# Output projection of a conv decoder block: a tile's three products become a 512- and a 256-column one, and VectorE adds the halves

## The chip, the cores and the metric

The kernel runs on one core of a Trainium2 chip, in one launch. The metric is the device time of that launch in microseconds; several runs of the kernel are timed, and their median counts. One further execution is taken by the hardware profiler, and all rows below are from it.

## The reference, cut to what matters

One decoder layer over 256 tokens of width 2048, in float32. The condition c gives six modulation vectors (sh1, sc1, g1, sh2, sc2, g2). The part that the change touches is the end of the convolution mixer and the start of the second normalisation:

```
u = jax.nn.silu(_layer_norm(u, ln_g, ln_b))
y = u @ w_out + b_out
x = x + (1.0 + g1[:, None, :]) * y
h = _rms_norm(x, norm2_g[i]) * (1.0 + sc2[:, None, :]) + sh2[:, None, :]
u = jnp.square(jax.nn.relu(h @ mlp_w1[i]))
x = x + (1.0 + g2[:, None, :]) * (u @ mlp_w2[i])
```

## The kernel before

**Precision.** A float32 product is made of three products in a reduced float32 format (F32R). Weights and activations are both split into a high part, a rounded copy, and a low part, the remainder: high x high, high x low and low x high are added up. ScalarE makes the high part of the weights (L236), VectorE or GpSimd the low part (L240). A weight tile is 128 x 128; a split works on half of 16 such tiles at a time, and six buffers each are there for high and low halves (`hi`, `lo`). The activations lie as `hl`, channels on the partitions, with the 256 tokens' high parts in columns 0 to 255 and their low parts in 256 to 511.

**Stages.** The kernel goes through a list of jobs: 16 jobs ("in", i) of the input projection with the convolution, 8 jobs ("out", i) of the output projection, and then the feed-forward part in four quarters of jobs ("up", ...), ("down", ...). A job ("out", i) makes the output channels of two tiles, c = 0 and c = 1, and for each of them runs over 16 tiles k of the inner dimension.

**Products.** `mm` has two forms. The plain one (L268, L269) makes a 512-column product of the high weights with high and low activations side by side, and a 256-column product of the low weights with the high activations; the sum then lies in two halves of 256 columns that have yet to be added. The merged one (L264 to L266) makes three 256-column products into the same 256 columns. Job ("out", 0) has a form of its own (`mm_pair`, L283 to L286), jobs 1 to 7 are merged, and job ("up", 0, 0) is plain with `xa` in place of `hl`.

**Accumulators.** PSUM tiles come from named pools: `acc` and `mm` have two buffers each, `small` and `row` one each. A buffer of `acc` holds 512 columns. In jobs 1 to 7 it holds both tiles c of one job.

**What follows an output job.** ScalarE scales each tile by 1 + g1 and adds the bias `gb` = (1 + g1) b_out (L1419), VectorE adds the pair to x (L1420), ScalarE squares the new x (L1422) and scales it by the second norm's factors (L1431), and `split_act` splits the result for the first "up" job (ScalarE L251, VectorE L254). GpSimd sums the squares (L1427).

**Other work of the stage.** After each job stand 1 to 3 columns of the modulation (sh2, L665: two products of 128 x 1024 with an accumulated sum; others L669) on VectorE. Their second half reads a copy of the condition in PSUM that ScalarE makes (L1441). GpSimd makes the low weight parts for jobs 0 to 5, VectorE those for 6 and 7. The first "up" job also has 64 small products (L600) into `row`, ahead of its last two k.

**Order.** Each engine has one queue and takes its instructions in the order written. A scheduler sets that order from its own estimate of the times and from priorities (`urgent()`) and explicit constraints (`tc.issue_after`). Loads of weights and modulation rows are issued by SyncE into seven buffers `raw`, each as soon as its buffer is free.

Of the kernel before, what the change touches and what calls it, by code (L numbers as in the profile page):

```python
# [9 lines left out]
F32 = mybir.dt.float32  # L10
F32R = mybir.dt.float32r
AF = mybir.ActivationFunctionType
ALU = mybir.AluOpType
PSUM = bass.MemoryType.PSUM

P = 128
T = 256
# [18 lines left out]
SH1, SC1, G1, SH2, SC2, G2 = range(6)  # L36
# [51 lines left out]
def conv_block(ctx: ExitStack, tc: tile.TileContext, x, vec, dwq, c_row, mod_r, mod_t, mod_c, w_first, w_in, w_out, w1, w2, out):  # L88
    nc = tc.nc
# [6 lines left out]
    ps = ctx.enter_context(tc.tile_pool(name="ps", bufs=2, space=PSUM))  # L96
# [17 lines left out]
    xs = start_pool.tile([P, KT, T], F32, name="x0")  # L114
# [16 lines left out]
    for i in range(2):  # L131
        p = ps.tile([P, 2, 2 * T], F32, name="mm", bufs=2)
# [6 lines left out]
    state = {"used": 0}  # L139
# [3 lines left out]
    amps = {w: const.tile([P, KT], F32, name=f"amp{w}") for w in (SC1, SC2)}  # L143
# [8 lines left out]
    def urgent():  # L152
        return tc.high_priority(offset=URGENT)

    HALF = KT // 2
# [100 lines left out]
    def mm(p, c, key, acts_of, ks=range(KT), merged=False):  # L256
        halves = parts[key]
        for k in ks:
            hi, lo = halves[k // HALF]
            m = acts_of[k // 2][:, k % 2, :]  # L260
            if merged:
                out_p, begin, end = p[:, c, 0:T], k == 0, k == KT - 1
                w = hi[:, k % HALF, :]
                nc.tensor.matmul(out_p, w, m[:, 0:T], start=begin, stop=False)  # L264
                nc.tensor.matmul(out_p, w, m[:, T : 2 * T], start=False, stop=False)  # L265
                state["mm_end"] = nc.tensor.matmul(out_p, lo[:, k % HALF, :], m[:, 0:T], start=False, stop=end)  # L266
                continue
            nc.tensor.matmul(p[:, c, :], hi[:, k % HALF, :], m, start=(k == 0), stop=(k == KT - 1))  # L268
            state["mm_end"] = nc.tensor.matmul(  # L269
                p[:, c, T : 2 * T], lo[:, k % HALF, :], m[:, 0:T], start=False, stop=(k == KT - 1),  # L270
                skip_group_check=True,
            )
# [25 lines left out]
    def mm_tokens(sums, job, acts_of, last):  # L298
        steps = [(k, r) for k in range(HALF) for r in sums]
        if last:  # L300
            steps = [(k, r) for r in sums for k in range(HALF)]
        for k, (t, cs, p) in steps:
            hi, lo = [w[:, 4 * (k % 2) : 4 * (k % 2) + 4, :].rearrange("p k n -> p (k n)")[:, cs]
                      for w in parts[job + (k // 4,)][k // 2 % 2]]
            at = HALF * (job[2] % 2) + k
            m = acts_of[at // 2][:, at % 2, :]
            shared = job[0] == "down" and job[1] in EIGHT
            begin, end = at == 0 or shared and job[2] == 1 and t == 1 and at == HALF, at == KT - 1
            p_hi, p_lo = [m[:, n : n + P] for n in (t * P, T + t * P)]
            nc.tensor.matmul(p, p_hi, hi, start=begin, stop=False, skip_group_check=shared)  # L310
            nc.tensor.matmul(p, p_hi, lo, start=False, stop=False, skip_group_check=shared)  # L311
            nc.tensor.matmul(p, p_lo, hi, start=False, stop=end, skip_group_check=shared)  # L312

    def run_tasks():
        state["job"] += 1
        with tc.issue_after(state["w_lo"]), tc.issue_after(state["w_hi"]):
            for task in tasks.pop(state["job"], []):
                task()
# [371 lines left out]
    def mcol(which, k):  # L690
        return modc[:, which * KT + k : which * KT + k + 1]
# [21 lines left out]
    def ps_two():  # L713
        return ps.tile([P, 2, T], F32, name="acc", bufs=2)

    def two():
        return tmp.tile([P, 2, T], F32, name="two", bufs=6)

    def pair_of(tiles, k2):
        if tiles is xs:  # L720
            return xs[:, 2 * k2 : 2 * k2 + 2, :]
        return tiles[k2 // 2][:, 2 * (k2 % 2) : 2 * (k2 % 2) + 2, :]
# [4 lines left out]
    hl = [None] * HALF  # L727
# [81 lines left out]
    def splits(job):  # L809
        if job[0] == "eight":  # L810
            with urgent():
                split_eight(*job[1:])
            return
        if job[0] == "seven":
            with urgent():
                split_seven(*job[1:])
            return
        for c in range(2):
            if job + (c,) in parts_early:
                continue  # L820
            on_pool = job[0] == "in" or job in POOLED
            with urgent(), behind(c):
                split_w(job + (c,), nc.gpsimd if on_pool else nc.vector)
            if c == 0:
                state["next_hi"] = state["w_hi"]
                if job[0] in ("up", "down"):
                    with urgent():
                        run_tasks()

    def evac(p, cs=slice(0, 2), out=None):  # L830
        t1 = two()[:, cs, :]
# [7 lines left out]
    p = ps.tile([P, 512], F32, name="small", bufs=1)  # L839
# [10 lines left out]
    with urgent():  # L850
        part = two()[:, 0, :]
        nc.scalar.activation(part, p[:, 0:T], AF.Copy)
        p = ps.tile([P, 512], F32, name="row", bufs=1)
# [8 lines left out]
    for _ in range(2):  # L862
        p = ps.tile([P, 2, 2 * T], F32, name="mm", bufs=2)
# [52 lines left out]
    for k in range(KT):  # L916
        c = k % 2
# [261 lines left out]
    for n, job in enumerate(jobs):  # L1179
# [16 lines left out]
        kind, i = job[0], job[-1]  # L1196
# [32 lines left out]
                    top_up()  # L1229
            continue  # L1230
        if kind == "out" and i > 0:
            p = ps_two()
        elif not by_tokens(job):
            p = ps.tile([P, 2, 2 * T], F32, name="mm", bufs=2)
        if by_tokens(job) and (i % 2 == 0 or kind == "down" and job[1] in EIGHT and i < 4):
# [2 lines left out]
        if job == ("up", 0, 0):  # L1238
            mm(p, 0, job + (0,), xa, range(SIDE))
            for at in range(2 * UNSCALED):  # L1240
                shift_row(at, shown.pop(("up", 0, at // 2, at % 2)))
            fold_shift()
            mm(p, 0, job + (0,), xa, range(SIDE, KT))
            mm(p, 1, job + (1,), xa)
        elif job == ("out", 0):
            for k2 in range(HALF):
                with tc.issue_after(state["row_end"].ins) if k2 == 1 else ExitStack():
                    mm_pair(p, job, k2)
                if k2 == 0:
                    with tc.issue_after(state["mm_end"].ins):  # L1250
                        mod_chunk(*last_row[0][1:], last_row[1])
        elif job in K_OUTER:
            for k2 in range(HALF):
                for c in range(2):
                    mm(p, c, job + (c,), xa if plain else hl, range(2 * k2, 2 * k2 + 2))
        elif kind == "in":
            rows = [key for key in after[job] if key[0] != "col"] if i < KT - 1 else []
            for c in range(2) if i < KT - 1 else (1, 0):
                for ks in (range(HALF), range(HALF, KT)):
                    with tc.issue_after(state.pop("rows_end")) if "rows_end" in state else ExitStack():  # L1260
                        mm(p, c, job + (c,), hl, ks, i == KT - 1)
            if not CONV_AT.get(n):
                with tc.issue_after(state["mm_end"].ins):
                    mods(rows)
                state["rows_end"] = state["row_end"].ins
        elif by_tokens(job):
            mm_tokens(sums[kind, i // 2], job, u2 if kind == "down" else hl, n == len(jobs) - 1)
        else:
            for c in range(2):
                mm(p, c, job + (c,), hl, merged=kind == "out")  # L1270
        with tc.issue_after(state["mm_end"].ins) if kind == "in" else ExitStack():
            mod_finish()
        if n == KT - 3:
# [9 lines left out]
        if kind == "in":  # L1283
# [67 lines left out]
            gb = x_pool.tile([P, KT], F32, name="gb")  # L1351
# [18 lines left out]
            for k2 in range(HALF):  # L1370
# [17 lines left out]
                with urgent():  # L1388
                    nc.gpsimd.tensor_tensor(e, pair_of(cvs, k2), spread(mu), op=ALU.subtract)
                    state["e_end"] = nc.vector.tensor_tensor(e, e, spread(r), op=ALU.mult).ins  # L1390
                    for c in range(2):
                        k = 2 * k2 + c
# [17 lines left out]
        if kind == "out":  # L1410
            if i == 0:
                xs = take(("x", 0))
            t2 = p[:, :, 0:T]
            xp = pair_of(xs, i)
            with urgent():
                for c in range(2):
                    k = 2 * i + c
                    with tc.issue_after(state["next_hi"]) if i == HALF - 2 else ExitStack():
                        nc.scalar.activation(t2[:, c, :], t2[:, c, :], AF.Identity, scale=mcol(G1, k), bias=gb[:, k : k + 1])  # L1419
                nc.vector.tensor_tensor(xp, t2, xp, op=ALU.add)  # L1420
            ss = two()
            nc.scalar.activation(ss, xp, AF.Square)  # L1422
            if i == 0:
# [1 line left out]
            elif i < HALF - 1:  # L1425
                for c in range(2):
                    nc.gpsimd.tensor_tensor(sqacc, sqacc, ss[:, c, :], op=ALU.add)  # L1427
            a = two()
            for c in range(2):
                k = 2 * i + c  # L1430
                nc.scalar.activation(  # L1431
                    a[:, c, :], pair_of(xs, i)[:, c, :], AF.Copy, scale=amps[SC2][:, k : k + 1]
                )
            xa[i] = mp.tile([P, 2, 2 * T], F32R, name="u2", bufs=HALF)
            split_act(xa[i], a)
            if i == IN_PSUM[0]:
# [21 lines left out]
        elif kind == "up":  # L1458
# [7 lines left out]
            if plain:  # L1466
                with urgent():
                    t2 = evac(p)
                    a = two()
# [7 lines left out]
            elif not by_tokens(job):  # L1477
                with urgent():
                    t2 = evac(p)
                    a = two()  # L1480
# [115 lines left out]
```

## Time and profile before

| | |
|---|---|
| time, median of 3 runs | 1066.34 us (1066.32 to 1066.46) |
| the profiled execution's own time | 1066.46 us |
| its span, first to last instruction | 1064.7 us |
| TensorE / VectorE / ScalarE / GpSimd busy | 98% / 86% / 56% / 21% |
| mean granted TensorE clock | 0.997 |

The output jobs take some 85 us of the span, from about 297 to 381 us. A row of the time lines gives the start and length in microseconds; equal instructions in a row are merged (x4), and the time that the engine was idle before it stands in brackets with what ended it. The length of one instruction overlaps the next, so the pace is read from start to start.

### The profile page before, as it was taken

The page shows a single profiled execution, that of the slowest core. Times are in us where ns is not written, and L with a number is a line of the kernel's source. Part 1 is how long each engine was busy: PE and PEld are TensorE (multiplying, and loading weights), DVE is VectorE, ACT ScalarE, POOL GpSimd, SP SyncE. Part 2 cuts the span into 40 slices and gives each one's busy share as a digit, 9 for nine tenths or more (in the row PEclk, how much of TensorE's full clock was granted, in tenths as well). Part 3 has the DMA queues.
Part 4 walks back from the last instruction along what each step waited for, and adds up shares of the span by engine and source line. Part 5 has one row for each costly group of instructions (what it writes and reads, how often), then busy time and mean ns, then how long its engine had stood idle before and what let it go on. Part 6 is the DMA issues. An engine that isn't in the chain of part 4 may idle for free.

```text
span 1064.7 us, 15463 instructions
## 1 busy us (share of the span) xinstructions
PE 1046.3 (98%) x5776; PEld 865.1 (81%) x5776; DVE 911.7 (86%) x1191; ACT 601.5 (56%) x831; POOL 222.3 (21%) x153
## 2 busy tenths in 40 slices
PE   6999999999999999999999999999999999999998
PEld 3888886678699988888888888888888888888886
DVE  5777789998766889878799899899999899899996
ACT  4111298866775585344546565745566744656751
POOL 0000078989689272000000000000000000000001
PEclk8999999999999999999999999999999999999999
DMA  9999997996999976999996998693989796899853
GB/s 381 421 420 420 415 419 315 356 396 237 404 399 406 409 259 261 322 312 327 320 327 248 340 277 271 240 388 108 366 244 321 249 335 179 290 282 347 216 148 59
DMA packets 154333, 330.99 MB, mean 311 GB/s; under 512 B 88465, under 2 KB 114321, under 8 KB 119313
## 3 DMA queue, kind: packets, MB, share of 16 engines
q1 hardware_dynamic: 153248, 328.30, 85.1%
q0 software_dynamic: 864, 1.57, 1.1%
q8 instruction: 45, 0.74, 0.3%
q14 instruction: 30, 0.25, 0.1%
q10 hardware_dynamic: 146, 0.13, 0.0%
HBM read 313.71 MB, written 17.83 MB: 311 GB/s over the span
## 4 chain that ended last, share of the span: by engine, by line
PE 83%; DMA 10%; DVE 5%; ACT 1%; issue 1%; SPq 0%; DVEq 0%; ACTq 0%
PE mm L311 12%; PE mm L312 12%; PE mm L310 12%; DMA raw<-mod_c 9%; PE mm L268 6%; PE mm L269 3%; PE acc L265 3%; PE acc L264 3%; PE acc L266 3%; PE mm L1094 2%; PE row L576 2%; PE acc L485 2%; PE acc L486 2%; PE acc L484 1%; DVE raw L669 1%; DVE lo L240 1%
## 5 line engine op out<-in xcount | busy, mean ns | idle before, releaser
L236 ACT ACTIVATE hi<-raw 128x1024 fp32r<-128x1024 f32 x374 | 383.9, 1055 | 257.7 <-PE mm L312 127.6
L240 DVE TENSOR_TENSOR lo<-raw,hi 128x1024 fp32r<-128x1024 f32 x313 | 371.0, 1217 | 52.4 <-ACT hi L236 51.8
L240 POOL TENSOR_TENSOR lo<-raw,hi 128x1024 fp32r<-128x1024 f32 x61 | 155.8, 2581 | 30.1 <-ACT hi L236 29.8
L669 DVE SCALAR_TENSOR_TENSOR raw<-raw,cond 128x2048 f32<-128x2048 f32 x50 | 117.7, 2356 | 25.2 <-DMA raw<-mod_c 25.2
L460 POOL DMA_DIRECT2D out<-two x6 | 5.4, 902 | 639.2 <-DVE two L458 629.8
L311 PE MATMUL mm<-lo,u 128*128 128x512 f32 x320 | 124.5, 389 | 0.0
L312 PE MATMUL mm<-hi,u 128*128 128x512 f32 x320 | 124.0, 389 | 0.0
L310 PE MATMUL mm<-hi,u 128*128 128x512 f32 x320 | 123.8, 389 | 0.0
L310 PE MATMUL mm<-hi,hl 128*128 128x512 f32 x288 | 112.1, 389 | 0.0
L312 PE MATMUL mm<-hi,hl 128*128 128x512 f32 x288 | 112.1, 389 | 0.0
L311 PE MATMUL mm<-lo,hl 128*128 128x512 f32 x288 | 112.1, 389 | 0.0
L973 DVE SCALAR_TENSOR_TENSOR acc<-u,v,acc 128x256 f32<-128x256 f32 x230 | 91.5, 482 | 0.0
L268 PE MATMUL mm<-hl,hi 128*128 128x512 f32 x256 | 91.1, 399 | 0.0
L269 PE MATMUL mm<-hl,lo 128*128 128x256 f32 x256 | 71.7, 280 | 0.0
L310 PEld LDWEIGHTS mm<-hi,u 128*128 128x128 f32 x320 | 60.1, 188 | 12.6
L312 PEld LDWEIGHTS mm<-hi,u 128*128 128x128 f32 x320 | 60.1, 188 | 12.4
L311 PEld LDWEIGHTS mm<-lo,u 128*128 128x128 f32 x320 | 60.1, 188 | 12.4
L877 PE MATMUL mm<-two,first 128*128 128x256 f32 x240 | 56.7, 391 | 8.5 <-ACT two L935 8.5
L264 PE MATMUL acc<-hl,hi 128*128 128x256 f32 x224 | 63.4, 283 | 0.0
L265 PE MATMUL acc<-hl,hi 128*128 128x256 f32 x224 | 63.4, 283 | 0.0
L266 PE MATMUL acc<-hl,lo 128*128 128x256 f32 x224 | 63.4, 283 | 0.0
L310 PEld LDWEIGHTS mm<-hi,hl 128*128 128x128 f32 x288 | 54.1, 188 | 11.3
(383 smaller groups left out, 2018.8 us busy)
## 6 DMA issues: line engine op xcount, KB each, us to landing
raw<-w SPq DMA_DIRECT2D x128, 1024.0 KB, 7.6
raw<-mod_c SPq DMA_DIRECT2D x64, 1024.0 KB, 11.5
raw<-mod_r SPq DMA_DIRECT2D x28, 1024.0 KB, 8.7
raw<-w_in SPq DMA_DIRECT2D x16, 1024.0 KB, 10.6
raw<-w_out SPq DMA_DIRECT2D x16, 1024.0 KB, 8.2
first<-w_first SPq DMA_DIRECT2D x15, 1024.0 KB, 19.8
u<-kept SPq DMA_DIRECT2D x24, 512.0 KB, 7.6
flat<-two SPq DMA_DIRECT2D x30, 256.0 KB, 7.8
```

The costliest lines, as they stand in the source:

```text
L236: state["w_hi"] = nc.scalar.activation(hi, w[:, ks, :], AF.Copy).ins
L240: end = by.tensor_tensor(lo, w[:, ks, :], hi.bitcast(F32), op=ALU.subtract)
L264: nc.tensor.matmul(out_p, w, m[:, 0:T], start=begin, stop=False)
L265: nc.tensor.matmul(out_p, w, m[:, T : 2 * T], start=False, stop=False)
L266: state["mm_end"] = nc.tensor.matmul(out_p, lo[:, k % HALF, :], m[:, 0:T], start=False, stop=end)
L268: nc.tensor.matmul(p[:, c, :], hi[:, k % HALF, :], m, start=(k == 0), stop=(k == KT - 1))
L269: state["mm_end"] = nc.tensor.matmul(p[:, c, T : 2 * T], lo[:, k % HALF, :], m[:, 0:T], start=False, stop=(k == KT - 1), skip_group_check= ...
L310: nc.tensor.matmul(p, p_hi, hi, start=begin, stop=False, skip_group_check=shared)
L311: nc.tensor.matmul(p, p_hi, lo, start=False, stop=False, skip_group_check=shared)
L312: nc.tensor.matmul(p, p_lo, hi, start=False, stop=end, skip_group_check=shared)
L669: end = nc.vector.scalar_tensor_tensor(w, w, 1.0, cb, op0=ALU.mult, op1=ALU.mult, accum_out=acc)
L973: end = nc.vector.scalar_tensor_tensor(out, s, w, acc, op0=ALU.mult, op1=ALU.add)
```

## The change

Jobs ("out", 1) to ("out", 7) take the plain form of `mm`, with an accumulator buffer of `acc` for each tile c; job 0 is as before. In place of L1419 and L1420, VectorE adds each of the two halves of a tile to x, scaled by 1 + g1 (four L1423 a job). The bias is added to x by ScalarE ahead of that, after the job before (L1442). The scaled x (L1437) no longer goes to a buffer in SBUF but to `small` or `row` in PSUM, by turns. Two order constraints go.

```
@@ splits
-            if c == 0:
-                state["next_hi"] = state["w_hi"]
-                if job[0] in ("up", "down"):
-                    with urgent():
-                        run_tasks()
+            if c == 0 and job[0] in ("up", "down"):
+                with urgent():
+                    run_tasks()
@@ the jobs
         if kind == "out" and i > 0:
-            p = ps_two()
+            p = [ps_two().rearrange("p a t -> p (a t)")[:, None, :] for _ in range(2)]
...
+        elif kind == "out":
+            for c in range(2):
+                mm(p[c], 0, job + (c,), hl)
         else:
             for c in range(2):
-                mm(p, c, job + (c,), hl, merged=kind == "out")
+                mm(p, c, job + (c,), hl)
@@ after an output job
-            t2 = p[:, :, 0:T]
             xp = pair_of(xs, i)
             with urgent():
-                for c in range(2):
-                    k = 2 * i + c
-                    with tc.issue_after(state["next_hi"]) if i == HALF - 2 else ExitStack():
-                        nc.scalar.activation(t2[:, c, :], t2[:, c, :], AF.Identity, scale=mcol(G1, k), bias=gb[:, k : k + 1])
-                nc.vector.tensor_tensor(xp, t2, xp, op=ALU.add)
+                if i == 0:
...
+                for c in range(2) if i else ():
+                    for a in range(2):
+                        nc.vector.scalar_tensor_tensor(
+                            xp[:, c, :], p[c][:, 0, T * a : T * a + T], mcol(G1, 2 * i + c), xp[:, c, :],
+                            op0=ALU.mult, op1=ALU.add,
+                        )
...
-            a = two()
+            a = ps.tile([P, 2, T], F32, name=("small", "row")[i % 2], bufs=1)
             for c in range(2):
                 k = 2 * i + c
-                nc.scalar.activation(
-                    a[:, c, :], pair_of(xs, i)[:, c, :], AF.Copy, scale=amps[SC2][:, k : k + 1]
-                )
+                end = nc.scalar.activation(a[:, c, :], xp[:, c, :], AF.Copy, scale=amps[SC2][:, k : k + 1])
+            for c in range(2) if i + 1 < HALF else ():
+                k = 2 * i + 2 + c
+                x_next = pair_of(xs, i + 1)[:, c, :]
+                with tc.issue_after(end.ins):
+                    nc.scalar.activation(x_next, x_next, AF.Identity, bias=gb[:, k : k + 1])
```

Below, acc_2832 and acc_2970 are the accumulators of jobs 1 and 2 before; acc_2834 and acc_2835 are those of job 1 (c = 0, c = 1) in the changed kernel, acc_2944 that of job 2, c = 0.

VectorE after job 0, before the change (x1 is x; mm_2681 is job 0's sum; mm_2942 and mm_2944 are the two halves of the condition):

```order
L1420 TENSOR_TENSOR x1_2504<-mm_2681,x1_2504 128x512
L665 SCALAR_TENSOR_TENSOR raw_2548,rest2_2502<-raw_2548,mm_2944 128x1024
L665 SCALAR_TENSOR_TENSOR raw_2660,modc_116<-raw_2660,mm_2942 128x1024
L665 SCALAR_TENSOR_TENSOR raw_2660,rest2_2502<-raw_2660,mm_2944 128x1024
L254 TENSOR_TENSOR u2_2806<-two_2803,u2_2806 128x2x256
L1420 TENSOR_TENSOR x1_2504<-acc_2832,x1_2504 128x512
```

The same place of VectorE in the changed kernel (mm_2916 and mm_2918 are the halves of the condition now):

```order
L1420 TENSOR_TENSOR x1_2504<-mm_2681,x1_2504 128x512
L665 SCALAR_TENSOR_TENSOR raw_2548,rest2_2502<-raw_2548,mm_2918 128x1024
L1423 SCALAR_TENSOR_TENSOR x1_2504<-acc_2834,modc_116,x1_2504 128x256
L665 SCALAR_TENSOR_TENSOR raw_2660,modc_116<-raw_2660,mm_2916 128x1024
L665 SCALAR_TENSOR_TENSOR raw_2660,rest2_2502<-raw_2660,mm_2918 128x1024
L1423 SCALAR_TENSOR_TENSOR x1_2504<-acc_2834,modc_116,x1_2504 128x256
L1423 SCALAR_TENSOR_TENSOR x1_2504<-acc_2835,modc_116,x1_2504 128x256
```

The one addition of job 1 has become four, and the two of its c = 0 stand on either side of two L665.

TensorE from job 1 to job 2, before the change (hl_ are the activations, hi_ and lo_ the weight halves; in brackets the semaphores that the instruction waits for, named after the engine):

```order
L264 MATMUL acc_2832<-hl_2657,hi_2677 128x256
L265 MATMUL acc_2832<-hl_2657,hi_2677 128x256
L266 MATMUL acc_2832<-hl_2657,lo_2678 128x256
L264 MATMUL acc_2970<-hl_2586,hi_2814 128x256 [waits Activation_49]
L265 MATMUL acc_2970<-hl_2586,hi_2814 128x256
```

The same place of TensorE in the changed kernel:

```order
L268 MATMUL acc_2835<-hl_2657,hi_2677 128x512
L269 MATMUL acc_2835<-hl_2657,lo_2678 128x256
L268 MATMUL acc_2944<-hl_2586,hi_2816 128x512 [waits DVE_49,PE_49,Activation_49]
L269 MATMUL acc_2944<-hl_2586,lo_2817 128x256 [waits Pool_49]
L268 MATMUL acc_2944<-hl_2586,hi_2816 128x512
```

Job 2 begins in the buffer that job 1's c = 0 was in, and its first product waits for VectorE, on which job 2 before had no wait.

VectorE from job 5's c = 0 on, before the change (acc_3392 is the accumulator of job 5):

```order
L240 TENSOR_TENSOR lo_3389<-raw_3222,hi_3388 128x1024
L665 SCALAR_TENSOR_TENSOR raw_3226,modc_116<-raw_3226,mm_2942 128x1024
L665 SCALAR_TENSOR_TENSOR raw_3226,rest2_2502<-raw_3226,mm_2944 128x1024
L1420 TENSOR_TENSOR x1_2504<-acc_3392,x1_2504 128x512
L665 SCALAR_TENSOR_TENSOR raw_3230,modc_116<-raw_3230,mm_2942 128x1024
```

The same place of VectorE in the changed kernel (acc_3282 is job 5's c = 0, acc_3169 the c = 1 of job 4, u2_3247 job 4's scaled x):

```order
L1423 SCALAR_TENSOR_TENSOR x1_2504<-acc_3169,modc_116,x1_2504 128x256
L240 TENSOR_TENSOR lo_3275<-raw_3140,hi_3274 128x1024
L665 SCALAR_TENSOR_TENSOR raw_3144,modc_116<-raw_3144,mm_2916 128x1024
L665 SCALAR_TENSOR_TENSOR raw_3144,rest2_2502<-raw_3144,mm_2918 128x1024
L1423 SCALAR_TENSOR_TENSOR x1_2504<-acc_3282,modc_116,x1_2504 128x256
L254 TENSOR_TENSOR u2_3247<-small_3242,u2_3247 128x2x256
L240 TENSOR_TENSOR lo_3279<-raw_3140,hi_3278 128x1024
L665 SCALAR_TENSOR_TENSOR raw_3148,modc_116<-raw_3148,mm_2916 128x1024
L665 SCALAR_TENSOR_TENSOR raw_3148,rest2_2502<-raw_3148,mm_2918 128x1024
L1423 SCALAR_TENSOR_TENSOR x1_2504<-acc_3282,modc_116,x1_2504 128x256
```

Between the two additions of job 5's c = 0 stand an L254, an L240 and two L665 here.

## Rows read from the trace of the kernel before

**Rows 1.** The page, its first line and TensorE's busy time, share of the span.

```profile
span 1064.7 us, 15463 instructions
...
PE 1046.3 (98%) x5776; PEld 865.1 (81%) x5776; DVE 911.7 (86%) x1191; ACT 601.5 (56%) x831; POOL 222.3 (21%) x153
```

**Rows 2.** Busy time by stretch (stretch, length, engines, clock, DMA share, GB/s).

```profile
342.00:354.00 12.00, 12.00 (x102) 12.00 (x102) 11.97 (x17) 6.39 (x10) 8.99 (x7) 1.00 0.98 382
```

**Rows 3.** Waits from 296 to 394 us (total, times, longest).

```profile
ACT acc L1419 <- PE acc L266: 20.0, 5, 5.7
```

**Rows 4.** Time line of TensorE: a merged job, then the plain "up" job.

```profile
325.73 0.28 PE L266 MATMUL acc<-hl,lo 128*128 128x256 f32 x1
...
328.13 0.28 PE L265 MATMUL acc<-hl,hi 128*128 128x256 f32 x1
...
381.70 0.40 PE L268 MATMUL mm<-u,hi 128*128 128x512 f32 x1
...
385.86 0.40 PE L268 MATMUL mm<-u,hi 128*128 128x512 f32 x1
```

**Rows 5.** Time line of ScalarE: the condition's second half, ends of jobs 3, 7.

```profile
311.43 1.01 ACT L1441 ACTIVATE mm<-cond 128x1024 f32<-128x1024 f32 x1
...
335.05 1.11 ACT L1419 ACTIVATE acc<-acc,gb,modc 128x256 f32<-128x256 f32 x2 [4.71 <-PE acc L266]
...
381.13 1.11 ACT L1419 ACTIVATE acc<-acc,gb,modc 128x256 f32<-128x256 f32 x2 [1.34 <-PE acc L266]
```

**Rows 6.** Groups by form, 296 to 394 us (busy, mean ns, idle before).

```profile
L236 ACT ACTIVATE hi<-raw 128x1024 fp32r<-128x1024 f32 x35 | 35.6, 1049 | 8.5 <-PE acc L265 4.0 <-PE mm L283 3.4 <-PE mm L268 0.5
L665 DVE SCALAR_TENSOR_TENSOR raw<-raw,mm 128x1024 f32<-128x1024 f32 x24 | 28.1, 1211 | 2.5 <-ACT mm L1441 2.5
...
L240 DVE TENSOR_TENSOR lo<-raw,hi 128x1024 fp32r<-128x1024 f32 x12 | 14.0, 1218 | 0.3 <-ACT hi L236 0.3
...
L254 DVE TENSOR_TENSOR u<-two,u 128x512 fp32r<-128x512 f32 x8 | 12.2, 1523 | 7.3 <-ACT u L251 7.3
...
L1419 ACT ACTIVATE acc<-acc,gb,modc 128x256 f32<-128x256 f32 x14 | 7.5, 533 | 20.2 <-PE acc L266 20.0
L1431 ACT ACTIVATE two<-x,amp 128x256 f32<-128x256 f32 x16 | 7.2, 496 | 0.0
...
L251 ACT ACTIVATE u<-two 128x512 fp32r<-128x512 f32 x8 | 5.0, 626 | 0.1
L1422 ACT ACTIVATE two<-x 128x512 f32<-128x512 f32 x8 | 5.0, 622 | 3.0 <-DVE x L1420 3.0
L1420 DVE TENSOR_TENSOR x<-acc,x 128x512 f32<-128x512 f32 x7 | 4.8, 686 | 6.3 <-ACT acc L1419 6.3
...
L737 DVE SCALAR_TENSOR_TENSOR acc<-x,amp,small 128x256 f32<-128x256 f32 x5 | 2.3, 488 | 0.1
...
L254 DVE TENSOR_TENSOR hl<-acc,hl 128x512 fp32r<-128x512 f32 x2 | 1.4, 692 | 4.0 <-ACT hl L251 4.0
```

**Rows 7.** Time line of VectorE after job 0.

```profile
312.48 1.22 DVE L665 SCALAR_TENSOR_TENSOR raw<-raw,mm 128x1024 f32<-128x1024 f32 x1 [2.51 <-ACT mm L1441]
...
313.63 1.22 DVE L665 SCALAR_TENSOR_TENSOR raw<-raw,mm 128x1024 f32<-128x1024 f32 x1
```

**Rows 8.** Time line of TensorE at the end of the stage.

```profile
387.40 1.95 PE L600 MATMUL row<-raw,shz 128*32 128x128 f32 x64 [0.15 <-ACT shz L1453]
389.94 0.50 PE L268 MATMUL mm<-u,hi 128*128 128x512 f32 x1 [0.58 <-DVE u L254]
```

**Rows 9.** Time line of TensorE at the program's start.

```profile
20.14 5.53 PE L877 MATMUL mm<-two,first 128*128 128x256 f32 x16 [4.87 <-ACT two L935]
...
28.97 3.62 PE L877 MATMUL mm<-two,first 128*128 128x256 f32 x16
```

**Rows 10.** Busy time by stretch at the program's start, with the granted clock.

```profile
17.00:20.50 3.50, 0.36 (x1) 0.36 (x2) 3.31 (x8) 0.98 (x2) 0.00 (x0) 0.50 1.02 424
20.50:24.00 3.50, 3.50 (x9) 2.76 (x9) 3.46 (x5) 0.04 (x1) 0.00 (x0) 0.52 1.01 421
```

More of the change, by code (lines that the diff above doesn't have):

```diff
@@ L1412, in conv_block @@
                 xs = take(("x", 0))
-            t2 = p[:, :, 0:T]
             xp = pair_of(xs, i)
             with urgent():
-                for c in range(2):
-                    k = 2 * i + c
-                    with tc.issue_after(state["next_hi"]) if i == HALF - 2 else ExitStack():
-                        nc.scalar.activation(t2[:, c, :], t2[:, c, :], AF.Identity, scale=mcol(G1, k), bias=gb[:, k : k + 1])
-                nc.vector.tensor_tensor(xp, t2, xp, op=ALU.add)
+                if i == 0:
+                    t2 = p[:, :, 0:T]
+                    for c in range(2):
+                        nc.scalar.activation(t2[:, c, :], t2[:, c, :], AF.Identity, scale=mcol(G1, c), bias=gb[:, c : c + 1])
+                    nc.vector.tensor_tensor(xp, t2, xp, op=ALU.add)
+                for c in range(2) if i else ():
[4 more added lines that the diff above has]
+                        )
             ss = two()
```

## The prediction

> **What bounds the kernel now.** I read the page first: TensorE is busy for 98% of the span [rows 1]. A busy TensorE says nothing yet about one stage, so I turned to the stretch that the change touches, 296 to 394 us: the busy time by stretch, the waits, the groups by form, then the time lines of each engine.
>
> In the waits of that stretch ScalarE waits for TensorE's output products, 20.0 us in all [rows 3], and TensorE waits for VectorE only after the last of them [rows 8]. No engine there waits for a DMA. So the stage runs at TensorE's pace: the ends of the output jobs, where L1419 is released, lie at 335.05 and four jobs later at 381.13 [rows 5], 11.52 us apart, which is 32 products of three times 0.120 us [rows 4]. But VectorE is close behind: from 342 to 354 it was busy for 11.97 of 12.00 us [rows 2], and it takes its work in the written order. TensorE was free of it because a job's two sums share one accumulator of the two named acc, so a finished job could wait a whole job long, 11.52 us, to be read.
>
> **The change part by part.** *Pace.* Seven jobs of 32 weight tiles, 224 in all, go from three 256-column products to a 512- and a 256-column one. The columns are equal, 768. Twenty products of 256 columns take 2.40 us, from 325.73 to 328.13, so three take 0.360; the later stage already has the new pair, and twelve pairs take 4.16 us, from 381.70 to 385.86, so one takes 0.347 [rows 4]. That is 224 x 0.0133 = 3.0 us less. Both prices are measured at the full clock, so I give the term only 2.8 to 3.2.
>
> The Trainium skill, "TensorE: Matmul & The Clock Gate", section "Wait — 56ns, not 53.3ns?", speaks against this term: a matmul costs its columns over 2.4 GHz and about 2.5 ns. By it, one product fewer per tile would give an estimate of 224 x 2.5 ns = 0.6 us. The rows show 13 ns per tile and not 2.5, and I keep 3.0.
>
> *The accumulators.* Now each half job (one c) fills an accumulator of its own, so the two hold one job and not two. Job n's c = 0 must be read by two additions (L1423) before job n + 1 may begin, that is, within the 5.55 us (16 x 0.347) in which TensorE does c = 1. TensorE's first product of job 2 now waits for VectorE; before it waited for nothing on VectorE there. So what counts is where these additions stand in VectorE's order.
>
> *First place: job 2.* TensorE ended job 1 at 335.05 - 2 x 11.52 = 312.0; by the pace it now ends 0.4 earlier, at 311.6, and wants its c = 0 accumulator at once. VectorE's order after job 0's addition is: L665 on the second half of cond, an addition of job 1's c = 0, two more L665, and then the other addition. The first L665 waited in the trace for ScalarE's copy L1441, which began at 311.43 and took 1.01 us [rows 5], and started at 312.48 [rows 7]; ScalarE now has one activation of 0.5 us (L1431, [rows 6]) less ahead of that copy, so say 312.0. From there: L665 1.15 (start to start, [rows 7]), addition 0.49 (L737, the same instruction with a PSUM operand, took 488 ns [rows 6]), two L665 2.3, addition 0.49: 316.5. TensorE waits 316.5 - 311.6 = 4.9 us. Behind that product stands all of TensorE's work; ScalarE's and GpSimd's copies wait for TensorE to free their buffers. Bounds: if ScalarE's copy comes no earlier than before, 5.4; if additions and L665 overlap better than in the rows, 4.0.
>
> *Jobs 3, 4 and 5.* Two to four L665 stand between the additions, at most 4.6 us, under the 5.55. I take no wait.
>
> *Second place: job 6.* Count from the end of job 5's c = 0. VectorE's order is L240 on a tile whose high part ScalarE can copy only when TensorE is half through c = 0: 2.77 us before its end, plus the copy (L236) of 1.05 [rows 6], so L240 starts at -1.7 and ends at -0.5. Then two L665 to +1.8, the first addition to +2.3, L254 (0.69 with a PSUM source [rows 6], 0.61 to the next start) to +2.9, L240 to +4.0, two L665 to +6.3, the second addition to +6.8. TensorE wants the accumulator at +5.55: it waits 1.3 us. Bounds: 0, if VectorE has caught up, to 2.0. In job 7 only an L669 stands between; no wait.
>
> *The rest of VectorE and ScalarE.* VectorE gains 28 x 0.49 = 13.7 us of additions, loses 7 x 0.69 = 4.8 of L1420, and saves up to 8 x (1.52 - 0.69) = 6.6 on L254, whose source moves to PSUM [rows 6]: 2.3 us more, beside other work, save at the two places above. ScalarE trades 14 activations of 533 ns (L1419) for 14 biases that the trace lacks; between 496 (L1431) and 533 there is nothing to gain or lose. SyncE's order of loads stays through the stage. On GpSimd the sums of squares move by a place or two, ahead of low parts that TensorE needs a job later; I count them as nothing.
>
> *The end of the stage.* Before, TensorE waited 0.15 us ahead of L600 and 0.58 ahead of the product at 389.94 [rows 8], since L1419 and VectorE's queue delayed the last tile. Now one half is added while TensorE does the other, and after the last product come two additions, 1.0, and ScalarE's square, scale and copy, 0.62 + 0.50 + 0.63, and L254, 0.69 [rows 6]: 3.4 us, while TensorE still has some twelve pairs, 4.2 us, to do. L600 now waits for that L254, too, its buffer being the scaled x, and still finds it done. So 0.7 us goes; bounds 0 and 0.7.
>
> *The clock.* A wait of 4.9 us has one like it in the trace: TensorE idled for 4.87 us before 20.14 [rows 9], the granted clock was 0.50 in 17.0 to 20.5 and 0.52 in 20.5 to 24.0 (1.2 GHz of 2.4 [rows 10]), and the group that followed took 5.53 us against 3.62 for the same group later [rows 9]: 1.9 us. Bounds 0 and 1.9; I take 1.9, since that row is the nearest in length.
>
> **Sum.** -3.0 + 4.9 + 1.3 - 0.7 + 1.9 = +4.4 us on the profiled execution's own 1066.46 (its span of 1064.7 [rows 1] and 1.8 around it), 1070.9. The median lies 0.12 below that execution, so 1070.7. After the stage TensorE waited for hardly anything until the end, so I let the delay stand; scheduling is another there, and I allow 0.7 either way.
>
> **The rivals.** *The clock holds* (1068.8): all as above without the 1.9. For it: only one idle time of that size is in the trace, and one is no rule. Against it: the new one is as long. The Trainium skill, same page, section "What's actually happening", says that the monitor's window runs free of the kernel's start. By that rule the same gap may or may not lose the clock, which would make this rival about as likely as the forecast.
>
> *The first wait alone* (1067.5): the second place dissolves, as VectorE gained time in the first, and the clock holds, -3.0 + 4.9 - 0.7 = +1.2. For it: the second is short, and VectorE could do more while TensorE stood. Against it: its order is bound to TensorE's own ends.
>
> *VectorE becomes the bound* (1073.3): two more jobs wait as at job 6, 2 x 1.3 on top. For it: 11.97 of 12.00 busy [rows 2] before 2.3 us were added. Against it: the L665 between the additions come to less than 5.55 in the others.
>
> *The fixed cost per product is the page's 2.5 ns* (1073.1): the pace gives 0.6 in place of 3.0; against it stand [rows 4].
>
> *The other side: VectorE frees in time* (1062.6): if both additions of job 1's c = 0 are done by 311.6, nothing waits, and -3.0 - 0.7 = -3.7 remain. It decides at ScalarE's copy for the first L665: it would have to end 4.9 us earlier, at 307.1. In the trace it began at 311.43, behind job 0's own activations, which the change leaves. It is also what comes out if two accumulators turn out to be enough for a reason that I don't see in the order.
>
> **How the numbers follow.** Forecast 45%, its own range 1069.5 to 1072; clock holds 27%; first wait alone 8%; VectorE the bound 8%; fixed cost 2%; faster 10%. What a measurement of this kernel tells from no change is about 0.2%, 2.1 us: 1064.2 to 1068.5. The clock case lies 0.3 above that edge, and I count 16 of its 27 as slower. Slower: 45 + 8 + 2 + 16 = 71%; the same: 8 + 11 = 19%; faster 10%. The range of 1067.0 to 1072.5 leaves out the faster case and the two of 1073.
>
> **What would show it.** Pairs of products 0.347 us apart in the seven jobs; an idle time of about 4.9 us ahead of job 2's first product, released by VectorE's L1423; one of about 1.3 ahead of job 6's; a granted clock of about half after the first; L254 at 0.69; no idle time at the products after L600. I am wrong if TensorE never waits for L1423, or if the waits are at other jobs.

## The result and the profile after

The changed kernel takes 1072.91 us (median of 6 runs, 1070.47 to 1076.94); the kernel before, beside it, 1066.34 (1066.31 to 1066.82). The ratio is 1.0061 [1.0051, 1.0072]: slower by 0.6%. The forecast was 1070.7 with a range of 1067.0 to 1072.5: the direction is right, the size is 2.2 us short, 0.4 beyond the range. The profiled execution is the longest of the six, 1076.94 us.

The page after; TensorE is as good as always busy again, as in [rows 1], with a longer span:

```profile
span 1075.2 us, 15044 instructions
...
PE 1049.6 (98%) x5552; PEld 855.4 (80%) x5552; DVE 912.7 (85%) x1212; ACT 599.7 (56%) x831; POOL 218.1 (20%) x153
```

What TensorE waits for from 296 us to the end (engine and line, releaser: total, times, longest):

```profile
PE acc L268 <- DVE x L1423: 5.7, 2, 4.7
PE mm L312 <- DVE u L254: 2.6, 2, 1.9
```

The first line is the stage's: TensorE now waits for VectorE's additions, where before [rows 3] ScalarE waited for TensorE's products. The second was not in the forecast. The places stand in TensorE's time line (start, length, idle time before):

```profile
311.56 0.28 PE L269 MATMUL acc<-hl,lo 128*128 128x256 f32 x1
316.52 0.47 PE L268 MATMUL acc<-hl,hi 128*128 128x512 f32 x1 [4.68 <-DVE x L1423]
...
364.54 0.47 PE L268 MATMUL acc<-hl,hi 128*128 128x512 f32 x1 [1.04 <-DVE x L1423]
...
392.53 1.03 PE L695 MATMUL small<-two,ones 128*128 128x256 f32 x4
393.48 1.95 PE L600 MATMUL row<-raw,shz 128*32 128x128 f32 x64
395.37 0.50 PE L268 MATMUL mm<-u,hi 128*128 128x512 f32 x1
...
986.33 0.79 PE L312 MATMUL mm<-hi,u 128*128 128x512 f32 x1 [1.94 <-DVE u L254]
```

Job 2 begins at 316.52 and job 6 at 364.54, both behind an addition. At L600 and behind it, the idle times of [rows 8] are gone: the product behind L600 starts at 395.37, where before it started at 389.94. So the stage costs 5.4 us here; the other 5.1 of this execution's 10.5 came later.

VectorE in front of the first wait, to be read against [rows 7]:

```profile
312.07 1.22 DVE L665 SCALAR_TENSOR_TENSOR raw<-raw,mm 128x1024 f32<-128x1024 f32 x1 [2.12 <-ACT mm L1450]
313.22 0.48 DVE L1423 SCALAR_TENSOR_TENSOR x<-acc,modc,x 128x256 f32<-128x256 f32 x1
313.61 1.21 DVE L665 SCALAR_TENSOR_TENSOR raw<-raw,mm 128x1024 f32<-128x1024 f32 x1
...
314.75 1.22 DVE L665 SCALAR_TENSOR_TENSOR raw<-raw,mm 128x1024 f32<-128x1024 f32 x1
...
315.89 0.87 DVE L1423 SCALAR_TENSOR_TENSOR x<-acc,modc,x 128x256 f32<-128x256 f32 x2
```

The second addition of c = 0 comes behind three L665, and TensorE restarts with its end. Groups of the stage that answer to [rows 6], with the prices that were estimated there:

```profile
L1423 DVE SCALAR_TENSOR_TENSOR x<-acc,modc,x 128x256 f32<-128x256 f32 x28 | 13.3, 479 | 8.4 <-PE acc L269 8.1
...
L1442 ACT ACTIVATE x<-x,gb 128x256 f32<-128x256 f32 x14 | 6.4, 495 | 0.0
...
L254 DVE TENSOR_TENSOR u<-row,u 128x512 fp32r<-128x512 f32 x4 | 2.7, 686 | 5.0 <-ACT u L251 5.0
```

The granted clock behind the two longest waits (stretch, length, engines, clock, DMA share, GB/s):

```profile
317.10:320.50 3.40, 3.40 (x12) 2.82 (x12) 2.93 (x6) 0.43 (x1) 2.61 (x2) 0.50 1.01 422
...
986.20:989.50 3.30, 3.17 (x8) 2.49 (x9) 3.30 (x7) 0.00 (x0) 0.00 (x0) 0.50 1.00 420
```

Each is at 1.2 GHz. In the first, 12 products, 6 pairs, were begun, where a pair every 0.353 us gives 9.6; 16 pairs of job 2 took 7.25 us (316.52 to 323.77) in place of 5.65, which is 1.6 us.

The late wait at 986.33 is in a step that passes data through DRAM: `flat` is written there and read back turned. From the chain of work ahead of it (start, length, what):

```profile
947.66 8.65 DMA flat<-two
...
964.62 3.37 DMA two<-flat
...
971.67 6.58 DMA two<-flat
```

ScalarE's L541, which takes in the last read, shows it on its time line, before and after:

```profile
968.37 0.63 ACT L541 ACTIVATE two<-two 128x512 f32<-128x512 f32 x1 [1.75 <-DMA two<-flat]
```

```profile
978.27 0.63 ACT L541 ACTIVATE two<-two 128x512 f32<-128x512 f32 x1 [4.42 <-DMA two<-flat]
```

L541 is 9.9 us later now, with TensorE only 6.4 us behind just ahead of the wait (its L312 of 975.95 before starts at 982.37 here: 5.4 from the stage, 1.0 around a wait at 509 us). The other 3.5 were lost in the transfers; the trace does not show why. The late wait and the half clock behind it put TensorE another 4.0 us behind, which makes 10.4 in all.

### The profile page after: what moved, and what is told of

The parts are those of the page before. It is cut to its first block, busy times and chain, and to the rows that moved or that the text cites. A ratio compares the mean times of both kernels' runs of the same rounds, so it can differ in the third digit from the quotient of the medians.

```text
span 1075.2 us, 15044 instructions
## 1 busy us (share of the span) xinstructions
PE 1049.6 (98%) x5552; PEld 855.4 (80%) x5552; DVE 912.7 (85%) x1212; ACT 599.7 (56%) x831; POOL 218.1 (20%) x153
## 4 chain that ended last, share of the span: by engine, by line
PE 68%; DMA 16%; DVE 8%; SPq 3%; issue 3%; ACT 2%; DVEq 0%; ACTq 0%
DMA raw<-mod_c 10%; PE mm L312 9%; PE mm L310 9%; PE mm L311 9%; PE mm L268 6%; PE acc L268 4%; DMA flat<-two 3%; PE mm L269 3%; SPq L532 3%; PE acc L269 2%; DVE lo L240 2%; PE mm L1092 2%; PE row L576 2%; DVE raw L669 2%; DMA two<-flat 2%
## 5 line engine op out<-in xcount | busy, mean ns | idle before, releaser
L240 DVE TENSOR_TENSOR lo<-raw,hi 128x1024 fp32r<-128x1024 f32 x313 | 372.5, 1221 | 42.4 <-ACT hi L236 41.2
L240 POOL TENSOR_TENSOR lo<-raw,hi 128x1024 fp32r<-128x1024 f32 x61 | 151.3, 2504 | 30.9 <-ACT hi L236 29.9
L312 PE MATMUL mm<-hi,u 128*128 128x512 f32 x320 | 125.3, 393 | 2.6 <-DVE u L254 2.6
L312 PE MATMUL mm<-hi,hl 128*128 128x512 f32 x288 | 112.0, 389 | 0.0
L268 PE MATMUL acc<-hl,hi 128*128 128x512 f32 x224 | 81.0, 405 | 5.7 <-DVE x L1423 5.7
L312 PEld LDWEIGHTS mm<-hi,u 128*128 128x128 f32 x320 | 60.4, 189 | 16.2 <-DVE u L254 3.6
L312 PEld LDWEIGHTS mm<-hi,hl 128*128 128x128 f32 x288 | 54.1, 188 | 11.3
L310 PEld LDWEIGHTS mm<-hi,hl 128*128 128x128 f32 x288 | 54.1, 188 | 11.2
## 6 DMA issues: line engine op xcount, KB each, us to landing
raw<-w_in SPq DMA_DIRECT2D x16, 1024.0 KB, 10.5
```

The costliest lines, as they stand in the source:

```text
L240: end = by.tensor_tensor(lo, w[:, ks, :], hi.bitcast(F32), op=ALU.subtract)
```

## The experiments

Each was timed beside the kernel before (median 1066.36 to 1066.45 us in these); two of them are single executions.

**The changed kernel again.** No edit.

> The changed kernel once more. Its profile had waits of 4.7 us at job 2 and 1.0 at job 6, pairs 0.353 us apart in the stage, the clock at half for 3.4 us after the first wait, and two more waits long after the stage (0.7 us at 509 us, 1.9 us at 986 us, the clock at half again behind it). Theory (the stage costs a fixed 5.3 us; the late waits hang on when a load through DRAM lands and come and go): time 1070.5 to 1073.5, the waits at jobs 2 and 6 and the half clock behind the first are there again, those at 509 and 986 differ or are gone. Rival (the late waits belong to the changed order of instructions and are always there): 1076 to 1077 again, with 1.9 us at 986.

1072.3 us (1071.16 to 1072.76), 1.0054 [1.0042, 1.0067]: this second median lies inside the forecast's range, and the 0.4 beyond it is less than the two medians differ by. Its profile, of the 1071.16 us execution, has the 4.7 and 1.0 at jobs 2 and 6 and no other wait:

```profile
PE acc L268 <- DVE x L1423: 5.7, 2, 4.7
```

So the late waits are no fixed part. Two more profiles:

> The changed kernel, one more profile. The waits at jobs 2 and 6 and the stage's cost (4.7 to 5.3 us by the two profiles so far) are the same in every profile; what is later than that in the end is a wait at the products after the bounce through DRAM in the last quarter (L312, near 985 us: 1.94 us in one profile, none in the other). Theory (it hangs on when the transfers land, from run to run): a run of 1071 to 1071.5 shows no wait there, a run of 1072 to 1073 one of about 1 us. Rival (the stage's own cost varies): no wait there in any run, and the waits at jobs 2 and 6 or the pace of the pairs differ by 1 to 2 us.

> The changed kernel, one more profile, to the same question as the run before it: whether what this run has over 1071.1 to 1071.7 (the stage's 4.7 to 5.3 us) stands as a wait near 985 us, or in the stage.

TensorE's waits in the second and third of them (1072.58 and 1073.77 us):

```profile
PE acc L268 <- DVE x L1423: 5.9, 2, 4.7
PE acc L485 <- DVE lo L240: 0.5, 1, 0.5
PE mm L312 <- DVE u L254: 0.4, 1, 0.4
```

```profile
PE acc L268 <- DVE x L1423: 5.9, 2, 4.7
PE acc L485 <- DVE lo L240: 0.9, 1, 0.9
PE mm L312 <- DVE u L254: 0.2, 1, 0.2
```

In numbers (stage: the start of the product behind L600, less 389.94; rest: the execution's time less 1066.46 and less the stage):

| execution | stage | rest |
|---|---|---|
| 1076.94 | +5.4 | +5.1 |
| 1071.16 | +4.6 | +0.1 |
| 1072.58 | +4.7 | +1.5 |
| 1073.77 | +5.9 | +1.4 |

Neither theory holds alone: the stage differs by 1.3 us (0.3 of it from before the stage, whose first pair starts at 297.70 to 298.04) and the rest by 5. The last two have no wait at the place that I named, near 985 us; theirs are at 508 to 509 and at 577 to 579 us, the latter on VectorE's low halves. The +5.9 has the clock at half for twice as long:

```profile
315.90:322.50 6.60, 6.03 (x19) 5.20 (x20) 4.09 (x10) 2.96 (x6) 5.24 (x5) 0.50 1.02 423
```

**Columns behind the first additions.**

```
-            mods(after[job])
+            with tc.issue_after(state["first_added"]) if i in (1, 2) else ExitStack():
+                mods(after[job])
```

`first_added` is the second addition of job 1's c = 0.

> The changed kernel, with the L665 that stood before and between the two additions of job 1's c = 0 ordered behind them. Theory (a half job's accumulator is late by what VectorE has in front of its second addition): TensorE's wait at job 2's first product falls from 4.7 us to 2.0 to 2.6, what is left being ScalarE's bias (L1442 ended at 312.87); but four L665 now stand ahead of or between the additions of job 1's c = 1, and TensorE waits 2.5 to 3 us for them at job 2's c = 1: about the same sum, and with two times of half clock as after it, 1071 to 1074. If idle times of 2 to 3 us leave the clock alone, 1.7 less than the changed kernel. Rival (only the first place is tight): 2.5 us less than the changed kernel.

1071.53 us (1069.79 to 1072.51), 1.0045 [1.0033, 1.0058]. TensorE's time line:

```profile
314.02 0.47 PE L268 MATMUL acc<-hl,hi 128*128 128x512 f32 x1 [2.21 <-DVE x L1423]
322.25 0.58 PE L268 MATMUL acc<-hl,hi 128*128 128x512 f32 x1 [2.34 <-DVE x L1423]
```

The wait went from 4.68 to 2.21 and came back as 2.34 half a job later, where the four L665 now stand (2.5 to 3 were expected); a third, 0.58, is at job 6. The mechanism holds: what VectorE has ahead of the second addition sets the wait. The clock behind the two:

```profile
314.10:317.50 3.40, 3.40 (x19) 2.95 (x20) 3.40 (x7) 1.38 (x4) 3.40 (x4) 1.00 0.95 333
...
322.60:325.90 3.30, 3.30 (x12) 2.77 (x11) 2.26 (x4) 2.33 (x6) 3.22 (x3) 0.50 0.98 415
```

After 2.21 us idle it held, after 2.34 it was halved.

**Four accumulators.**

```
-            p = [ps_two().rearrange("p a t -> p (a t)")[:, None, :] for _ in range(2)]
+            if i % 2:
+                p = [ps_two().rearrange("p a t -> p (a t)")[:, None, :] for _ in range(2)]
+            else:
+                p = [ps.tile([P, 512], F32, name=name, bufs=1)[:, None, :] for name in ("small", "row")]
...
-            a = ps.tile([P, 2, T], F32, name=("small", "row")[i % 2], bufs=1)
+            a = two()
```

> The changed kernel with four accumulators: jobs 2, 4 and 6 sum into the buffers small and row, jobs 1, 3, 5 and 7 into the two of acc; the scaled x goes back to SBUF. Theory (the loss is the reuse of two buffers a half job after they were filled): no product waits for L1423, the clock stays at 1.00 through the stage, pairs stand 0.353 us apart; 224 x 0.0067 = 1.5 us less than before, and against it up to 2 us of waits for the low weight halves that VectorE makes for jobs 6 and 7 behind more work: 1064.5 to 1067. If pairs are at 0.347, 1.5 less. Rival (VectorE cannot carry the additions at all, whatever the buffers): waits of several us on VectorE remain, 1068 or more.

1066.07 us (1065.81 to 1067.74), 0.9998 [0.9989, 1.0007]. TensorE waits for no addition in its profile:

```profile
PE acc L269 <- DVE lo L240: 1.5, 1, 1.5
PE mm L312 <- DVE u L254: 0.6, 1, 0.6
```

The reuse of the buffers went, and with it 6 us. The edit also moves the scaled x back to SBUF; that its place in PSUM was not the cause is seen further on (two accumulators, another order), where it stays in PSUM and jobs 2 to 6 wait for no addition. Pairs stand 0.353 us apart, as expected; the 0.6 at the late L312 was not.

**A short wait in the kernel before.**

```
             p = ps_two()
+            if i == 2:
+                with urgent(), tc.issue_after(state["seen"]):
+                    nc.vector.memset(p, 0.0)
```

`seen` is the last L665 written so far.

> The kernel before (three 256-column products, everything else as before) with one addition: VectorE writes zeros to job 2's accumulator behind an L665, so that TensorE has to wait about 2 us at job 2's first product; the instructions after the stage stand in the order of before. It measures what a short wait there costs by itself. Theory (an idle time of about 2 us also loses the clock for 3.4 us, 1.6 us, as it did at 986): 1066.4 + 2.2 + 1.6 = 1070.2. Rival 1 (the wait alone): 1068.6. Rival 2 (later waits grow or shrink with the shift): more than 1071, or back at 1066 to 1067 with the delay taken up by slack later.

1069.6 us (1069.41 to 1070.66), 1.0032 [1.0019, 1.0045]: 3.2 us for a wait of 2.49, between the theory and the first rival. (The profile puts this wait down to ScalarE's L251, which ended at 314.31; VectorE's zeros ended at 314.20, and job 2 started at 314.35. Before, job 2 waited for nothing there.) The clock was halved behind it:

```profile
314.90:318.30 3.40, 3.40 (x19) 3.40 (x18) 3.40 (x7) 0.00 (x0) 3.40 (x3) 0.50 0.92 330
```

With 256-column products that costs less than I expected: 19 were begun where 0.120 us each gives 28, 1.1 us. And the 0.7 us of idle time at the end of the stage [rows 8] are gone behind it. The profiled execution, the longest, has a late wait too, 0.88 us at the L312 near 981 us, though VectorE, ScalarE and GpSimd have the order of before there (inside the stage a few places moved). So it comes without another order.

**The rest of the change without the two-product form.** Accumulators and `mm` as before, then

```
+                    nc.vector.scalar_tensor_tensor(
+                        xp[:, c, :], p[:, c, :], mcol(G1, 2 * i + c), xp[:, c, :], op0=ALU.mult, op1=ALU.add,
+                    )
```

> The rest of the change without its two-product form: three 256-column products a tile into one accumulator a job, as before; VectorE scales and adds each tile in one instruction, ScalarE adds the bias a job ahead, the scaled x lies in PSUM. Theory (only the accumulators that a half job takes cost time): no wait at jobs 2 or 6, 1066.4 within 0.6. Rival (the bias ahead and the moved scaling delay ScalarE or VectorE for others): waits of 1 to 3 us at the weight halves or at the end of the stage, 1067.5 to 1069.

1065.6 us (1065.31 to 1067.47), 0.9995 [0.9986, 1.0004]: these parts cost nothing. Its profile has no wait of TensorE in the stage, so the 0.15 and 0.58 at the end [rows 8] are gone with these parts alone; from 400 us on TensorE is 0.7 to 0.8 ahead of before, as the median is, though the interval does not tell this from nothing.

**Four accumulators and less for VectorE.**

```
-LATE_OUT = [1, 1, 2, 3, 3, 3, 1, 1]
+LATE_OUT = [1, 1, 3, 3, 3, 2, 2, 0]
...
-POOLED = [("out", i) for i in range(6)] + [("up", 0, 1), ("up", 0, 2)]
+POOLED = [("out", i) for i in range(7)] + [("up", 0, 1), ("up", 0, 2)]
```

> Four accumulators, and with them GpSimd makes the low weight halves of job 6, too, and one modulation column each is moved from jobs 4 or 5 to 3 or 6 and from 7 to 6 (1, 1, 3, 3, 3, 2, 2, 0 columns after the eight jobs). Theory (with four accumulators the time above the pace is the wait for low halves behind VectorE's other work, 1.5 us in that profile, and the last tile's): these waits go, 1066.1 - 1.5 - 0.6 = 1064.0, with pairs at 0.353 us; 1062.5 if they are at 0.347. Rival (GpSimd, 2.5 us for a half where VectorE needs 1.2, is late in VectorE's place): a wait of 1 to 3 us on GpSimd at job 7, 1066 to 1068.

1065.19 us (1064.85 to 1066.12), 0.9989 [0.9980, 0.9998], 1.2 slower than expected. The stage has no wait left, and TensorE leaves it 1.4 us ahead of before; 0.6 us stand at the late L312 again, and 0.9 of the 1.4 are lost there:

```profile
976.87 0.50 PE L312 MATMUL mm<-hi,u 128*128 128x512 f32 x1 [0.60 <-DVE u L254]
```

**Two accumulators, another order.**

```
+                        with tc.issue_after(gated.ins):
+                            nc.scalar.activation(x_next, x_next, AF.Identity, bias=gb[:, 2 + c : 3 + c])
...
+                        if c == 0:
+                            state["first_added"] = added.ins
...
-            mods(after[job])
+            with tc.issue_after(state["first_added"]) if i else ExitStack():
+                mods(after[job])
```

`gated` is the scaling of job 0, `added` an addition; L1429 below is L1423 here.

> The changed kernel with its two accumulators; only the order differs: the modulation columns of a job (L665) are ordered behind the two additions of that job's c = 0, and ScalarE adds job 1's bias directly behind its scaling of job 0. Theory (the loss came from what stood between the additions in VectorE's order, not from two buffers being too few): no product of jobs 2 to 6 waits for an addition; but VectorE's work is only put off, and the low halves that it makes for jobs 6 and 7 and the last tile are late in their turn: 3 to 5 us of waits at job 7 and at the end of the stage (L695, L600), 1066.4 - 1.5 + 4 = 1067 to 1070, and the clock at half behind a wait of over 2 us in some runs. Rival (two buffers are too few): waits for the additions remain at two or more jobs, 1071 or more.

1071.83 us (1070.57 to 1072.43), 1.0047 [1.0035, 1.0060]. TensorE's waits:

```profile
PE row L600 <- DVE u L254: 2.7, 1, 2.7
PE small L695 <- ACT two L1436: 1.4, 1, 1.4
PE acc L268 <- DVE x L1429: 0.9, 1, 0.9
```

No product of jobs 2 to 6 waits for an addition; the 0.9 is job 7's. The first wait and job 6's have become 4.1 us at the end of the stage, where the last tile comes behind the work that VectorE had put off; the clock was half from 389.6 to 396.2 on top, so the time is above the 1070 that I had expected.

**The same, with less for VectorE.** `range(7)` in POOLED, and LATE_OUT = [1, 1, 3, 3, 3, 2, 1, 1].

> As the run before, and VectorE is relieved: GpSimd makes the low halves of job 6, too, and one modulation column goes from job 5 to job 2 (1, 1, 3, 3, 3, 2, 1, 1 columns). Theory: the waits at job 7 and at the end go as well, with two accumulators: 1066.4 - 1.5 - 0.7 = 1064.2, up to 1066 with what the later stages take. Rival (two buffers are too few, or four are what made the kernel with GpSimd's job 6 fast): 1068 or more.

1064.47 us (1064.26 to 1064.94), 0.9981 [0.9972, 0.9990]: faster than both kernels, with two accumulators. The list of waits from 140 to 1060 us has none of TensorE. VectorE does all four additions of job 1 before TensorE wants either buffer:

```profile
309.89 0.99 DVE L1429 SCALAR_TENSOR_TENSOR x<-acc,modc,x 128x256 f32<-128x256 f32 x2
310.80 1.21 DVE L665 SCALAR_TENSOR_TENSOR raw<-raw,mm 128x1024 f32<-128x1024 f32 x1
...
311.97 1.00 DVE L1429 SCALAR_TENSOR_TENSOR x<-acc,modc,x 128x256 f32<-128x256 f32 x2
```

The first two are done at 310.88, ahead of the end of job 1 near 311.6. That relief alone, the same two lines in the kernel before:

> The kernel before with only what relieved VectorE in the fastest run so far: GpSimd makes the low halves of job 6, too, and the columns after the jobs are 1, 1, 3, 3, 3, 2, 1, 1. It tells what of that run's 2.0 us is the two-product form's. Theory (the stage of before is TensorE's, and it waits only 0.7 us at its end): at most 0.7 less, 1065.7 to 1066.5, so that 1.5 us or so are the form's. Rival (the relief of VectorE is the gain): 1064.5 as with the two-product form.

1067.1 us (1066.94 to 1067.77), 1.0007 [0.9998, 1.0016]. It gains nothing by itself: TensorE's 0.2 and 0.6 at the end of the stage are still there in its profile, with 0.4 more at L695. So the 2.0 us of the kernel of 1064.47 belong to the change, once nothing waits for it. Not all of them are the two-product form's: the rest of the change without it took 1065.6, which leaves some 1.1 by the medians to the form with its order and relief, where pairs at 0.353 us give 1.6. The two runs' intervals overlap, so this split is not shown beyond the noise.

## Why the prediction was right and wrong

**First wait: right.** 316.5 and 4.9 us forecast, 316.52 and 4.68 measured, step by step in the order that was read, and 4.68 in all four profiles. What stands between the additions causes it: moving it moved the wait, buffers of their own or another order removed it.

**Second wait: right.** 1.3 at job 6 forecast, 1.04 to 1.20 measured, and none at the jobs that were named as free.

**End of the stage: right.** The 0.15 and 0.58 are gone and L600 waits for nothing.

**Clock: right in kind.** Behind the 4.7 us wait it was halved in all four profiles, and 1.9 was forecast where 1.6 was measured for one such stretch; the 1.9 came from other products ([rows 9]), so its nearness is partly luck. One of four had two in a row, up to 322.5, which the bounds of 0 to 1.9 did not hold. The rival in which the clock holds is out.

**Pace: mis-sized, 3.0 forecast, 1.6 measured in the profiled execution.** The step "one takes 0.347 [rows 4]" took one of two paces for the pace. TensorE's time line in the stage after:

```profile
307.79 0.40 PE L268 MATMUL acc<-hl,hi 128*128 128x512 f32 x1
...
311.32 0.40 PE L268 MATMUL acc<-hl,hi 128*128 128x512 f32 x1
```

Ten pairs in 3.53 us are 0.353 each, and 224 x (0.360 - 0.353) is 1.6. The trace of before held this price, too, nine pairs in 3.18 us a few microseconds behind the rows that I used:

```profile
390.39 0.40 PE L268 MATMUL mm<-u,hi 128*128 128x512 f32 x1
...
393.57 0.40 PE L268 MATMUL mm<-u,hi 128*128 128x512 f32 x1
```

I read one stretch and bounded the term at 2.8 to 3.2 from it. In the other three profiles 64 to some 120 of the 224 pairs ran at 0.347, which makes the term 1.9 to 2.3. With 1.6, the same sum gives 1072.1.

**After the stage: wrong.** "I let the delay stand; scheduling is another there, and I allow 0.7 either way": the four profiles show 0.1, 1.4, 1.5 and 5.1 us there. That TensorE waited for hardly anything in one trace did not say how near the next releaser was: VectorE's time line of before has the L254 that the late L312 waits for:

```profile
975.69 0.68 DVE L254 TENSOR_TENSOR u<-shz,u 128x512 fp32r<-128x512 f32 x1
```

TensorE took it there without waiting:

```profile
977.53 0.39 PE L312 MATMUL mm<-hi,u 128*128 128x512 f32 x1
```

The L254 was done at 976.37, 1.2 us before, at the end of a chain in which one read took 6.58 us in another execution. A late start of TensorE is not needed to lose these 1.2 us: the late L312 also waited 0.63 and 0.60 us in the two kernels with four accumulators, where TensorE was 0.7 and 1.4 us ahead of before. In the thirteen profiles here the wait goes with the read: ScalarE's L541 near 970 us waited for it 4.42, 3.11, 2.73 and 1.88 us in the four that have the late wait, and 1.75 or less in the other nine. Nor does the scheduler's other order decide alone, since one order gave 0.1 to 5.1. Why the transfers land when they do stays open.

In the profiled execution the stage's terms close: -1.6 of pace, 4.85 and 1.2 for the waits from start to start, 1.6 of half clock and -0.7 at the end make 5.35, and 5.4 were measured. Against the 4.4 of the sum the stage was 0.2 to 1.5 us longer in the four profiles, and the rest, put at nothing within 0.7, was 0.1 to 5.1. The execution nearest to the median, 1072.58, has 0.3 and 1.5 of these: there the step after the stage is the larger part of the 2.2 us. Which is larger differs from run to run.

**The rivals.** Two come near in time by other mechanisms. "VectorE becomes the bound" (1073.3): no two more jobs waited. The fixed cost of 2.5 ns a product (1073.1): one product fewer saves 7 or 13 ns. "The first wait alone" is out by the wait at job 6, and the faster case by the first wait. The Trainium skill ("TensorE: Matmul & The Clock Gate", section "Wait — 56ns, not 53.3ns?") has 2.5; for these products the measurement decides.

## What to carry to other kernels

When an accumulator's life is cut from a job to half a job, go through the reader's queue in its written order: what stands between the last product and the last read is the wait, and it can be read off before anything runs. Put the reads first and take work off that engine: order alone moved the loss, relief alone gained nothing, both gave 1064.47. Read a price from several stretches of the trace, and ask of every later stage how early its releaser is, not only whether something waited.

## What the runs showed that was not expected

The pairs of products run at one of two paces, 0.3467 or 0.353 us, at a granted clock of 1.00 throughout, and changed over where TensorE started again after a wait or behind another product. The changed kernel again, on either side of job 6's wait:

```profile
360.28 0.40 PE L268 MATMUL acc<-hl,hi 128*128 128x512 f32 x1
...
362.40 0.40 PE L268 MATMUL acc<-hl,hi 128*128 128x512 f32 x1
...
363.96 0.47 PE L268 MATMUL acc<-hl,hi 128*128 128x512 f32 x1 [1.04 <-DVE x L1423]
...
364.73 0.39 PE L268 MATMUL acc<-hl,hi 128*128 128x512 f32 x1
...
369.93 0.40 PE L268 MATMUL acc<-hl,hi 128*128 128x512 f32 x1
```

Six pairs take 2.12 us before, 0.353 each; fifteen take 5.20 after, 0.3467. Another execution of the same kernel had it the other way round, and the profiled 1076.94 us one kept 0.353 over both waits. With the columns behind the first additions the change came near 376 us, behind one product of the next stage and 0.06 us of idle time. What chooses was not found.

The clock was halved behind waits of 1.94, 2.34 and 2.49 us and held behind one of 2.21, so length alone does not decide. The Trainium skill, same page, section "What's actually happening", says that the monitor runs free of the kernel's start, so that the change depends on where the work falls; these four fit that, and none of them shows it.
